# Where the squares of x lie, when the row of norms is laid out, and three small changes of order and banks, in a fused attention block

## The chip, the core and the metric

The kernel runs on one core of a Trainium2 chip. The metric is the device time of one execution in microseconds, median of the runs. TensorE multiplies matrices into the banks of PSUM; ScalarE (ACT), VectorE (DVE) and GpSimd (POOL) work on tiles in SBUF, the first two on PSUM too; SyncE (SP), ScalarE and GpSimd issue DMA transfers.

## The reference

All inputs are float32: 512 positions, model width 1024, 16 heads of 64.

```python
h = rms_norm(x, norm_g)
proj = h @ w_in                     # fq fk fv fz | mq mk mv mz | ga gb | fl
q, k = rms_norm(heads(fq), fox_q_g), rms_norm(heads(fk), fox_k_g)
y_fox = fox_attention(q, k, heads(fv), log_sigmoid(fl + b_f)) * silu(fz)
q, k = rope(rms_norm(heads(mq), moba_q_g)), rope(rms_norm(heads(mk), moba_k_g))
y_moba = moba_attention(q, k, heads(mv)) * silu(mz)
merged = sigmoid(ga + b_gate[0]) * (y_fox @ w_fox) + sigmoid(gb + b_gate[1]) * (y_moba @ w_moba)
return x + merged @ w_out
```

`rms_norm` divides by the root of the mean square plus 1e-6. Both attentions are causal over the 512 positions.

## The kernel before

Every large product is made of three matmuls on split operands: a left and a right operand are each cut into a rounded high part and a low part (`hi`, `lo`; `Gh`, `Gl`; `Zh`, `Zl`), and high by high, high by low and low by high are added in PSUM. ScalarE makes the high part of a tile with a copy, VectorE the low part with a subtraction.

PSUM has eight banks, handed out under tags: `pj` (2 banks), `tp` (3), `lg` (2) and `pv` (1). In SBUF the tag `y` has 15 tiles of 128x512 and the tag `u` has 4. A tile of a tag waits until the oldest one under that tag is free.

The stages, in order of time:

- **Start.** Input tiles of x transposed (`xt`, tag `y`) and the first weights are loaded on SP's queue. Meanwhile TensorE runs `WARM` matmuls on a tile of zeros (L107). Then come two projections that need no norm of x: `first_qk("fqa")` into two `pj` and two `lg` banks, and `first_qk("fka")` into three `tp` banks and `pv`. Each has eight steps `kk` over the inner dimension, with 12 matmuls a step.
- **Norms of x.** `x_stats` (L221) loads x untransposed in eight tiles of 128x512, squares each on ScalarE with a running sum per row (`ms2`), and makes `r`, one over the root, with three small VectorE steps and a power on GpSimd. `norm_row` (L237) lays `r` out as a row over the free dimension (`rbc`) with four transposes on TensorE. `normalise` (L243) multiplies the `xt` tiles with it and splits them into `Gh`, `Gl`.
- **fz gates** (`pz_fza`, `pz_fzb`, L405 to L407), the value projection `fva`, then four attention groups with four heads each. A group is a list of steps `Tr`, `Aa` (logits and exponentials), `Bb` (transposed probabilities times values) and a last step `Yp(1)`, called `gate` in the main loop, which multiplies the group's second pair of heads with its gate and splits it. It is run inside the next group. Projections of later groups (`pj_...`, `pz_...`, `pf`) are woven between the steps as filler.
- **Gates and merging**, with half-size products in a Strassen-like scheme, and at last the output projection, seven products that share sums in the banks `b[1]` to `b[4]` (`product`, L925; `keep`, `result`, L942 to L958). `result` adds the x it needs and sends the rows out: one transfer per tile, and for the very last tile two halves, the second on SP's queue.

The program is written in this order, and a scheduler orders each engine's instructions by its own costs; `issue_after` holds a few back. Each engine runs its list strictly in order. DMA transfers from ScalarE and SP go round eight semaphores: a transfer waits until the one eight places before it has landed.

In the main loop, the step list of a group is put together so:

```python
    for n in range(4):
        ...
        inter(body + ([following] if n < 3 else []) + tail, fill)
        if n < 3:
            body, tail = nxt[1][:1] + gate + nxt[1][1:], nxt[2]
            gate = nxt[3]
```

Of the kernel before, what the change touches and what calls it, by code (L numbers as in the profile page):

```python
# [9 lines left out]
AF = mybir.ActivationFunctionType  # L10
OP = mybir.AluOpType
# [5 lines left out]
NT = S // P  # L17
KT = D // P
HD = 64
CW = 256  # L20
EPS = 1e-6
NEG = -3.0e38
WARM = 8
WR = 4

C_NG, C_BG, C_FQ, C_FK, C_MQ, C_MK, C_BF, C_GQ, C_GK, C_END = 0, 8, 24, 25, 26, 27, 28, 36, 52, 68
# [3 lines left out]
def fox_moba_kernel(ctx: ExitStack, tc, xT, x, w_in, w_fl, w_fox, w_moba, w_out, cst, rope, out):  # L30
# [3 lines left out]
    V, A, G, T = nc.vector, nc.scalar, nc.gpsimd, nc.tensor  # L34
# [182 lines left out]
    r = con.tile([P, NT], F32, name="r")  # L217
# [3 lines left out]
    def x_stats():  # L221
        G.memset(mh, -0.5)
        for t in range(NT):
            for hf in range(2):
                xt = t2("y", 15, f"x{t}{hf}")
                nc.sync.dma_start(out=xt, in_=x[t * P:(t + 1) * P, hf * 512:(hf + 1) * 512])
                j = t2("u", 4, "junk")
                A.activation(j, xt, AF.Square, accum_out=ms2[:, t, hf:hf + 1])
        V.tensor_add(mm, ms2[:, :, 0], ms2[:, :, 1])
        V.tensor_scalar(mm, mm, 1.0 / D, EPS, op0=OP.mult, op1=OP.add)  # L230
        V.tensor_scalar(e2, mm, EPS, None, op0=OP.mult)
        G.tensor_tensor(out=r, in0=mm, in1=mh[:, :NT], op=OP.pow)
# [634 lines left out]
    def group_o():  # L867
        R, B, b, e = {}, {}, {}, {}
        base = len(preps)

        def src(key, c):
            k0, n0 = 4 * (int(key[0]) - 1) + 2 * c, 2 * (int(key[1]) - 1)
            return w_out[n0:n0 + 2, :, k0:k0 + 2, :].rearrange("n p k c -> p n (k c)")

        def wide(t):
            return t.rearrange("p a b -> p (a b)")[:, 0:1024]

        def dst(key, c):
            return wide(R[key, c]).rearrange("p (n k) -> p n k", n=2)

        def load(key, c, pool=sb):
            tag, bufs = ("wr", WR) if pool is sb else ("wx", 4)
            R[key, c] = pool.tile([P, 4, CW], F32, name=f"wr_o{key}{c}", tag=tag, bufs=bufs)
            nc.sync.dma_start(out=dst(key, c), in_=src(key, c))

        def minus(key, c, plus):
            A.activation(R[key, c], R[key, c], AF.Copy, scale=-1.0)  # L887
            G.dma_start(out=dst(key, c), in_=src(plus, c), accum_op=OP.add)  # L888

        def sub(key, c, x, y):  # L890
            V.tensor_tensor(out=wide(R[key, c]), in0=wide(R[x, c]), in1=wide(R[y, c]), op=OP.subtract)

        def prep(n, c):

            def go():
                key = ("11", "21", "22", "12", "22", "11", "21")[n]
                if (n, c) == (2, 0):
                    hi, lo = (stage["pool"].tile([P, 4, CW], F32R, name=f"w{q}_o{n}{c}") for q in "hl")
                else:
                    hi, lo = (sb.tile([P, 4, 264], F32R, name=f"w{q}_o{n}{c}", tag=f"w{q}", bufs=4) for q in "hl")  # L900
                A.activation(wide(hi), wide(R[key, c]), AF.Copy)  # L901
                V.tensor_tensor(out=wide(lo), in0=wide(R[key, c]), in1=wide(hi).bitcast(F32), op=OP.subtract)  # L902
                B[n, c] = [wide(t).rearrange("p (n k c) -> p n k c", n=2, c=CW) for t in (hi, lo)]
                if n == 0:
                    minus("11", c, "12")
            return go
        for key in ("11", "21"):
            for c in range(2):
                loads.append((lambda key=key, c=c: load(key, c), base + 13))
        groups["prep"] = lambda n, cs=(0, 1): [prep(n, c)() for c in cs]  # L910

        def late_loads():
            for key in ("22", "12"):
                for c in range(2):
                    load(key, c, stage["pool"])
            for c in range(2):
                minus("12", c, "22")

        def left_o(what, k, t):
            if what[0] == "S":  # L920
                return [so(what, q)[:, k, t * P:(t + 1) * P] for q in range(2)]
            t0 = HT * (int(what[1]) - 1) + t * P
            return [z[:, t0:t0 + P] for z in MG[4 * (int(what[2]) - 1) + k]]

        def product(n):  # L925
            what, _, at = O_PRODUCTS[n]
            new = at not in b
            if new:
                b[at] = [pst(tg, nb, f"po{at}{t}") for t, (tg, nb) in enumerate(
                    {1: (("lg", 2), ("lg", 2)), 2: (("tp", 3), ("tp", 3)), 3: (("pj", 2), ("pj", 2)),  # L930
                     4: (("tp", 3), ("pv", 1))}[at])]
            for t in range(2):
                o = b[at][t].rearrange("p (n c) -> p n c", n=2)
                for k in range(4):
                    hi, lo = B[n, k // 2]
                    gh, gl = left_o(what, k, t)
                    r = k % 2
                    T.matmul(o, gh, hi[:, :, r, :], start=(new and k == 0), stop=False, skip_group_check=True)  # L938
                    T.matmul(o, gh, lo[:, :, r, :], start=False, stop=False, skip_group_check=True)  # L939
                    T.matmul(o, gl, hi[:, :, r, :], start=False, stop=(k == 3), skip_group_check=True)  # L940

        def keep(at, tq, cq):  # L942

            e[at] = sb.tile([P, 2, S], F32, name=f"eo{at}", tag="qk", bufs=4)
            for t in range(2):
                A.activation(e[at][:, t, :], b[at][t], AF.Copy)
                t0 = tq * HT + t * P
                G.dma_start(out=e[at][:, t, :], in_=x[t0:t0 + P, cq * 512:(cq + 1) * 512], accum_op=OP.add)

        def result(bb, ee, tq, cq, parts=1):  # L950
            for t in range(2):
                o = t2("u", 4, "ot")
                t0 = tq * HT + t * P
                n = 512 // (parts if t else 1)
                for c in range(0, 512, n):
                    V.tensor_tensor(out=o[:, c:c + n], in0=b[bb][t][:, c:c + n], in1=e[ee][:, t, c:c + n], op=OP.add)
                    eng = nc.scalar if c == 0 else nc.sync
                    eng.dma_start(out=out[t0:t0 + P, cq * 512 + c:cq * 512 + c + n], in_=o[:, c:c + n])  # L958

        def evac(n):  # L960
            if n == 0:
                keep(1, 0, 0)
            elif n == 1:
                result(2, 1, 0, 0)
            elif n == 2:
                keep(4, 0, 1)
            elif n == 3:
                keep(3, 1, 1)
            elif n == 4:
                b[6] = b[1]  # L970
                keep(6, 1, 0)
            elif n == 5:
                pass
            else:
                result(3, 6, 1, 0, 2)

        groups["out"] = result
        groups["product"], groups["evac"] = product, evac
        groups["sub"] = lambda *key: [sub(key[0], c, *key[1:]) for c in range(2)]
        groups["WO"] = late_loads  # L980
# [52 lines left out]
    load_fl("fka", COLS["fka"], 0)  # L1033
    load_fl("fka", COLS["fka"], 1)
    b1 = first_qk("fqa", (("pj", 2), ("pj", 2), ("lg", 2), ("lg", 2)))
    b2 = first_qk("fka", (("tp", 3), ("tp", 3), ("tp", 3), ("pv", 1)))
    x_stats()
    for t in range(NT):
        evac_qk(b1[t], "fqa", t)
    for t in range(NT):  # L1040
        evac_qk(b2[t], "fka", t)
    forget_exp()
    norm_row()
    pump(0)
    fz = filler(["fza", "fzb"])
    for k, u in enumerate(fz):
# [14 lines left out]
    for n in range(4):  # L1061
        nxt = []

        def following(n=n, nxt=nxt):
            br, half, cq, ck = plan[n + 1][:4]
            if n == 1:
                moba_begin()
            nxt.extend(attn_group(br, half, col(cq), col(ck)))
            nxt[0][0]()
        fill = filler(plan[n][4])  # L1070
        if n == 0:
            for k in range(4):
                store = []

                at = 3 * k + 5

                def with_sums(u=fill[at], k=k, store=store):
                    u()
                    with tc.issue_after(last_on(mybir.EngineType.DVE)):
                        store.append(make_sums(k))  # L1080

                def with_store(u=fill[at + 1], store=store):
                    u()
                    store[0]()
                fill[at], fill[at + 1] = with_sums, with_store
        inter(body + ([following] if n < 3 else []) + tail, fill)
        if n < 3:
            body, tail = nxt[1][:1] + gate + nxt[1][1:], nxt[2]
            gate = nxt[3]
    seq(["wf3"])  # L1090
    enter("gates")
# [127 lines left out]
```

## Time and profile before

| | |
|---|---|
| median of 3 runs | 426.72 us (426.54 to 426.73) |
| profiled execution | 427.16 us, its span 425.3 us |
| TensorE busy | 418.5 us, 98% of the span |
| VectorE, ScalarE, GpSimd busy | 327.2, 271.4, 98.4 us |
| granted TensorE clock | 1.00 |
| DMA | 58.21 MB, mean 137 GB/s |

The profile gives for each engine the instructions in order of time: start and length in microseconds, engine, line of the kernel, operation, output and inputs by name, shape, count, and in brackets the time for which the engine sat idle before it and what ended that. A matmul's length includes the way through the array, so matmuls in a stream overlap; the distance between their starts is their pace. Rows of windows give, for a stretch of time, its length, then for TensorE, its weight loads, VectorE, ScalarE and GpSimd the busy time and the number of instructions, then the granted clock, the DMA share and GB/s. Rows of waits give the waiting engine and tile, what ended the wait, the total, the count and the longest. A row of one line of the kernel has the smallest, median and largest duration in ns and the first and last start.

### The profile page before, as it was taken

To read this page: it belongs to the slowest core of one execution; us is meant where nothing else is said; L and a number is where in the kernel's file an instruction comes from. 1 tells how busy PE (TensorE), PEld (TensorE's weight loads), DVE (VectorE), ACT (ScalarE), POOL (GpSimd) and SP (SyncE) were. 2 spreads that over 40 slices of the span, in tenths; PEclk is the share of its full clock that TensorE was granted. 3 is DMA by queue.
4 is the path that set the end of the run, shared out by engine and by line. 5 is a ranking of instruction groups with operands and counts; after the bars stand their busy time and mean duration, and the time that the engine had idled before them with its cause. 6 is when DMAs were issued, how large, how long until landed. Compare 5 with 4: busy or idle time off the path is not lost.

```text
span 425.3 us, 7669 instructions
## 1 busy us (share of the span) xinstructions
PE 418.5 (98%) x2887; PEld 387.7 (91%) x2887; DVE 327.2 (77%) x570; ACT 271.4 (64%) x514; POOL 98.4 (23%) x120
## 2 busy tenths in 40 slices
PE   7999999999999999999999999999999999999996
PEld 6998899999999998899998878899999989988884
DVE  5669976769979769568767698767979698689973
ACT  4975436776868867568746687655656535686450
POOL 1048200225132850025750102140000000022140
PEclk9999999999999999999999999999999999999999
DMA  7981144235576334304124222463052603696484
GB/s 243 398 308 55 52 146 139 58 124 175 168 221 217 85 99 125 96 29 125 38 88 124 79 70 72 201 225 123 25 176 65 229 5 112 220 245 116 99 140 158
DMA packets 25621, 58.21 MB, mean 137 GB/s; under 512 B 3064, under 2 KB 7856, under 8 KB 25584
## 3 DMA queue, kind: packets, MB, share of 16 engines
q1 hardware_dynamic: 13392, 38.11, 27.3%
q10 hardware_dynamic: 8800, 11.21, 8.7%
q0 software_dynamic: 3392, 8.39, 8.5%
q8 instruction: 23, 0.38, 0.3%
q14 instruction: 14, 0.11, 0.1%
HBM read 48.11 MB, written 6.32 MB: 128 GB/s over the span
## 4 chain that ended last, share of the span: by engine, by line
PE 96%; DVE 2%; DMA 1%; issue 0%; ACT 0%; SPq 0%; DVEq 0%; ACTq 0%
PE pb_GB L753 3%; PE pb_GA L753 3%; PE pb_GB L750 3%; PE pb_GA L750 3%; PE pb_GB L752 3%; PE pb_GA L752 3%; PE po L939 3%; PE po L938 3%; PE po L940 3%; PE pv L611 2%; PE pv L610 2%; PE lg L556 2%; PE lg L555 2%; PE pm L681 2%; PE pm L680 2%; PE pm L679 2%
## 5 line engine op out<-in xcount | busy, mean ns | idle before, releaser
L560 ACT ACTIVATE p<-p,negm 128x128 f32<-128x128 f32 (+1 forms) x64 | 35.7, 559 | 9.8 <-DVE negm L558 8.6
L558 DVE CUSTOM_DVE_ANT_0 p<-lg,mask 128x128 f32<-128x128 f32 (+1 forms) x64 | 30.9, 485 | 14.3 <-PE lg L556 13.7
L334 POOL TENSOR_TENSOR ff<-ss,mh 128x8 f32<-128x8 f32 x16 | 26.7, 1678 | 65.2 <-DVE ss L332 64.7
L888 POOL DMA_DIRECT2D wr_o<-in_w_out_dram x4 | 4.9, 1293 | 95.5 <-ACT wr_o L887 95.5
L136 DVE TENSOR_TENSOR wl_GA<-wr_ga,wh_GA 128x1024 fp32r<-128x1024 f32 x14 | 17.8, 1288 | 5.8 <-ACT wh_GA L134 3.7
L901 ACT ACTIVATE wh_o<-wr_o 128x1024 fp32r<-128x1024 f32 x14 | 14.8, 1059 | 10.0 <-PE pb_GB L752 2.8
L134 ACT ACTIVATE wh_GB<-wr_gb 128x1024 fp32r<-128x1024 f32 x14 | 14.6, 1059 | 9.5 <-PE pm L680 3.5
L134 ACT ACTIVATE wh_GA<-wr_ga 128x1024 fp32r<-128x1024 f32 x14 | 14.6, 1059 | 9.3 <-PE pb_GA L752 4.6
L555 PE MATMUL lg<-KH,QS 128*128 128x128 f32 (+1 forms) x64 | 20.5, 329 | 0.0
L902 DVE TENSOR_TENSOR wl_o<-wr_o,wh_o 128x1024 fp32r<-128x1024 f32 x14 | 16.9, 1221 | 3.8 <-ACT wh_o L901 3.8
L136 DVE TENSOR_TENSOR wl_GB<-wr_gb,wh_GB 128x1024 fp32r<-128x1024 f32 x14 | 16.9, 1222 | 3.5 <-ACT wh_GB L134 3.5
L636 DVE TENSOR_TENSOR ypair<-pv,ysh 64x512 f32<-64x512 f32 x16 | 11.0, 688 | 11.0 <-ACT ysh L635 10.8
L607 DVE TENSOR_TENSOR ptl<-p_a,pth 128x512 fp32r<-128x512 f32 x16 | 11.0, 685 | 4.6 <-ACT pth L606 4.5
L529 DVE SCALAR_TENSOR_TENSOR QS<-p_qT,cs,QS 64x512 fp32r<-64x512 f32 x16 | 12.0, 750 | 2.5 <-ACT QS L528 2.1
L635 ACT ACTIVATE ysh<-pv 64x512 f32<-64x512 f32 x16 | 9.5, 593 | 6.7 <-PE pv L611 5.6
L753 PE MATMUL pb_GA<-Gh,wl_GA 128*128 128x256 f32 x48 | 13.6, 283 | 0.0
L752 PE MATMUL pb_GA<-Gl,wh_GA 128*128 128x256 f32 x48 | 13.5, 281 | 0.0
L750 PE MATMUL pb_GA<-Gh,wh_GA 128*128 128x256 f32 x48 | 13.5, 281 | 0.0
L753 PE MATMUL pb_GB<-Gh,wl_GB 128*128 128x256 f32 x48 | 13.5, 281 | 0.0
L752 PE MATMUL pb_GB<-Gl,wh_GB 128*128 128x256 f32 x48 | 13.4, 281 | 0.0
L679 PE MATMUL pf<-yhf,wh_wf 128*128 128x512 f32 x32 | 13.1, 408 | 0.4 <-DVE zs_mzb L425 0.4
L528 ACT ACTIVATE QS<-p_qT,cs 64x512 fp32r<-64x512 f32 x16 | 10.9, 681 | 3.8 <-PE lg L555 2.0
(458 smaller groups left out, 1785.9 us busy)
## 6 DMA issues: line engine op xcount, KB each, us to landing
wr_ga<-in_w_in_dram SPq DMA_DIRECT2D x8, 512.0 KB, 3.7
wr_gb<-in_w_in_dram SPq DMA_DIRECT2D x8, 512.0 KB, 5.1
wr_o<-in_w_out_dram SPq DMA_DIRECT2D x8, 512.0 KB, 5.1
xt<-in_xT_dram SPq DMA_DIRECT2D x8, 256.0 KB
x<-in_x_dram SPq DMA_DIRECT2D x8, 256.0 KB, 6.3
KH<-KH ACTq DMA_DIRECT2D x16, 128.0 KB, 2.4
s_dramh<-sum_sh ACTq DMA_DIRECT2D x8, 256.0 KB
s_draml<-sum_sl ACTq DMA_DIRECT2D x8, 256.0 KB, 3.6
```

The source lines that it names most:

```text
L134: A.activation(hi[:, :, 0:n], src, AF.Copy)
L136: eng.tensor_tensor(out=lo[:, q, 0:n], in0=src[:, q], in1=hi[:, q, 0:n].bitcast(F32), op=OP.subtract)
L334: G.tensor_tensor(out=f2, in0=ss.rearrange("p t h -> p (t h)"), in1=mh, op=OP.pow)
L555: T.matmul(lg[:, :n], qs[:, qt], kh[:, :n], start=True, stop=False)
L558: V.tensor_tensor_reduce(pt, lg[:, :n], mask[:, 512 - n:512], -0.125, 3.0e38, op0=OP.add, op1=OP.min, accum_out=mkn[:, hh, i:i + 1])
L560: A.activation(pt, pt, AF.Exp, bias=mkn[:, hh, i:i + 1], scale=-1.0, accum_out=rs[:, hh, i:i + 1])
L679: T.matmul(p, hi[:, k, cc], yh, start=(k == 0), stop=False)
L750: T.matmul(o, hi[:, k, cc], lh, start=(n < 3 and c == 0 and k == 0), stop=False, skip_group_check=True)
L752: T.matmul(o, hi[:, k, cc], ll, start=False, stop=False, skip_group_check=True)
L753: T.matmul(o, lo[:, k, cc], lh, start=False, stop=(k == 3), skip_group_check=True)
L901: A.activation(wide(hi), wide(R[key, c]), AF.Copy)
L902: V.tensor_tensor(out=wide(lo), in0=wide(R[key, c]), in1=wide(hi).bitcast(F32), op=OP.subtract)
```

## The change

- `WARM` is 10 instead of 8.
- In `x_stats` the Square writes over the tile that it reads, so the scratch tile `junk` (tag `u`) is gone; the last two of the eight tiles of x take tag `u` instead of `y`.
- `norm_row()` is called before `first_qk("fka")` instead of after the evacuation of both projections and `forget_exp`.
- In the output projection, the second tile of bank 3 becomes two half tiles in two banks (the third from tag `tp`): its 12 matmuls of 512 columns in each of the two products become 24 of 256 columns, first half and then second half. `keep` and `result` read the halves from their banks.
- `gate` is put behind the second step of the next group's body instead of behind the first.

```diff
-WARM = 8
+WARM = 10
...
             for hf in range(2):
-                xt = t2("y", 15, f"x{t}{hf}")
+                xt = t2("u", 4, f"x{t}{hf}") if t == NT - 1 else t2("y", 15, f"x{t}{hf}")
                 nc.sync.dma_start(out=xt, in_=x[t * P:(t + 1) * P, hf * 512:(hf + 1) * 512])
-                j = t2("u", 4, "junk")
-                A.activation(j, xt, AF.Square, accum_out=ms2[:, t, hf:hf + 1])
+                A.activation(xt, xt, AF.Square, accum_out=ms2[:, t, hf:hf + 1])
...
-                    {1: (("lg", 2), ("lg", 2)), 2: (("tp", 3), ("tp", 3)), 3: (("pj", 2), ("pj", 2)),
+                    {1: (("lg", 2), ("lg", 2)), 2: (("tp", 3), ("tp", 3)), 3: (("pj", 2), ("pj", 2), ("tp", 3)),
                      4: (("tp", 3), ("pv", 1))}[at])]
-            for t in range(2):
-                o = b[at][t].rearrange("p (n c) -> p n c", n=2)
+
+            for t, c in ((0, slice(0, 2)),) + (((1, slice(0, 1)), (1, slice(1, 2))) if at == 3 else ((1, slice(0, 2)),)):
+                o = b[at][t + c.start].rearrange("p (n c) -> p n c", n=2)[:, 0:c.stop - c.start, :]
                 for k in range(4):
...
-                    T.matmul(o, gh, hi[:, :, r, :], start=(new and k == 0), stop=False, skip_group_check=True)
+                    T.matmul(o, gh, hi[:, c, r, :], start=(new and k == 0), stop=False, skip_group_check=True)
...
             for t in range(2):
-                A.activation(e[at][:, t, :], b[at][t], AF.Copy)
+                if at == 3 and t:
+                    for c in range(2):
+                        A.activation(e[at][:, t, c * CW:(c + 1) * CW], b[at][t + c][:, :CW], AF.Copy)
+                else:
+                    A.activation(e[at][:, t, :], b[at][t], AF.Copy)
...
-                    V.tensor_tensor(out=o[:, c:c + n], in0=b[bb][t][:, c:c + n], in1=e[ee][:, t, c:c + n], op=OP.add)
+                    V.tensor_tensor(out=o[:, c:c + n], in0=b[bb][t + 1][:, :n] if c else b[bb][t][:, :n], in1=e[ee][:, t, c:c + n], op=OP.add)
...
     b1 = first_qk("fqa", (("pj", 2), ("pj", 2), ("lg", 2), ("lg", 2)))
-    b2 = first_qk("fka", (("tp", 3), ("tp", 3), ("tp", 3), ("pv", 1)))
     x_stats()
     for t in range(NT):
         evac_qk(b1[t], "fqa", t)
+    norm_row()
+    b2 = first_qk("fka", (("tp", 3), ("tp", 3), ("tp", 3), ("pv", 1)))
     for t in range(NT):
         evac_qk(b2[t], "fka", t)
     forget_exp()
-    norm_row()
...
-            body, tail = nxt[1][:1] + gate + nxt[1][1:], nxt[2]
+            at = 2
+            body, tail = nxt[1][:at] + gate + nxt[1][at:], nxt[2]
             gate = nxt[3]
```

More of the change, by code (lines that the diff above doesn't have):

```diff
@@ L937, in product @@
                     r = k % 2
-                    T.matmul(o, gh, hi[:, :, r, :], start=(new and k == 0), stop=False, skip_group_check=True)
-                    T.matmul(o, gh, lo[:, :, r, :], start=False, stop=False, skip_group_check=True)
-                    T.matmul(o, gl, hi[:, :, r, :], start=False, stop=(k == 3), skip_group_check=True)
+                    T.matmul(o, gh, hi[:, c, r, :], start=(new and k == 0), stop=False, skip_group_check=True)
+                    T.matmul(o, gh, lo[:, c, r, :], start=False, stop=False, skip_group_check=True)
+                    T.matmul(o, gl, hi[:, c, r, :], start=False, stop=(k == 3), skip_group_check=True)
         def keep(at, tq, cq):
```

## The prediction

> **What bounds the kernel now.** I read the page's busy shares and its chain first, then TensorE's waits, then the windows of the first microseconds and of the end.
>
> ```profile
> span 425.3 us, 7669 instructions
> PE 418.5 (98%) x2887; PEld 387.7 (91%) x2887; DVE 327.2 (77%) x570; ACT 271.4 (64%) x514; POOL 98.4 (23%) x120
> PE 96%; DVE 2%; DMA 1%; issue 0%; ACT 0%; SPq 0%; DVEq 0%; ACTq 0%
> ```
>
> TensorE is busy for 98% of the span and carries 96% of the chain that ended last. So a change counts only if it alters the number or the pace of matmuls, opens or closes a gap in their stream, or moves the stretch behind the last one. The gaps are few:
>
> ```profile
> PE warm_ps L107 <- DVE fg_pre L471: 1.5, 1, 1.5
> PE fqa L382 <- ACT Zh L125: 0.7, 1, 0.7
> PE pf L679 <- DVE zs_mzb L425: 0.4, 1, 0.4
> PE p_b L600 <- DVE ptl L607: 0.2, 1, 0.2
> ```
>
> Besides 2.8 us of gaps there are 3.9 us after the last matmul and, hidden inside "busy", the slow pace at the start:
>
> ```profile
> 6.04:9.50 3.46, 3.46 (x16) 3.46 (x17) 3.17 (x6) 2.56 (x4) 0.00 (x0) 1.00 1.02 355
> 9.50:19.00 9.50, 9.50 (x82) 9.50 (x82) 7.54 (x12) 8.19 (x18) 0.00 (x0) 1.00 1.05 397
> 421.40:425.30 3.90, 0.00 (x0) 0.00 (x0) 0.76 (x2) 0.00 (x0) 0.00 (x0) 1.00 0.25 87
> ```
>
> The first entry after the length is TensorE's busy time with its matmuls. In 6.04 to 9.50 it is full with 16 matmuls of 256 columns, 0.216 us each; from 9.50 it is full with 82, 0.116 us each. TensorE ran at about half pace until then, though the granted clock (third from the end) reads 1.00 in both rows. These rows show the turn:
>
> ```profile
> 1.55 3.78 PE L107 MATMUL warm_ps<-warm 128*128 128x512 f32 x8 [1.55 <-DVE fg_pre L471]
> 6.04 0.58 PE L382 MATMUL fqa<-wh_fqa,Zh 128*128 128x256 f32 x1 [0.71 <-ACT Zh L125]
> 9.20 0.41 PE L382 MATMUL fqa<-wh_fqa,Zh 128*128 128x256 f32 x1
> 9.41 0.36 PE L383 MATMUL fqa<-wl_fqa,Zh 128*128 128x256 f32 x1
> 9.61 0.29 PE L382 MATMUL fqa<-wh_fqa,Zh 128*128 128x256 f32 x1
> 19.06 0.53 PE L382 MATMUL fka<-wh_fka,Zh 128*128 128x264 f32 x3
> 30.75 0.39 PE L405 MATMUL pz_fza<-Zh,wh_fza 128*128 128x512 f32 x1
> ```
>
> **Ten warm matmuls instead of eight.** Eight take 1.55 to 5.33, about 0.43 us each (0.21 us per 256 columns, doubled). Two more end at 5.33 + 0.86 = 6.19, while the first real matmul cannot start before 6.04. Their own cost is therefore at most 0.15 us, and less, since a matmul starts before the one ahead has drained. What they fill is the gap of 0.71 us. The fast pace came at about 9.57, some 3.5 us after the gap; the 3.78 us of work before the gap had not brought it. If it takes one stretch of 3.4 us or so without a hole, at fixed places in time, then the stretch before the one that ended at 9.57 ran from about 2.75 to 6.16 and had the gap in it. Without the gap the pace would double at 6.16.
>
> [...]
>
> What an early turn is worth is set by the operands:
>
> ```profile
> 6.59 0.75 DVE L126 SCALAR_TENSOR_TENSOR Zl<-xt,cs,Zh 128x512 fp32r<-128x512 f32 x1
> 9.04 1.43 DVE L126 SCALAR_TENSOR_TENSOR Zl<-xt,cs,Zh 128x512 fp32r<-128x512 f32 x2
> ```
>
> In the changed program's built order, step 0 has 8 matmuls before the first that needs Zl0. At 0.117 us they are issued by 6.98; Zl0 is ready at 7.34, so the other four run 7.4 to 7.9. Step 1's twelve end at 9.3. In step 2 the third matmul already needs Zl2, ready at 9.04 + 0.75 = 9.79, so it starts at 9.84. From there 70 matmuls of this group remain: 9.84 + 70 x 0.117 = 18.0, where the second group starts at 19.06 now. I take 0.1 us off for the two restarts: **-0.9 us** (bounds -1.1 and 0).
>
> **Mean squares and the row of norms.** These are not on TensorE's path, but they could get there.
>
> ```profile
> 19.20 1.07 SPq L226 DMA_DIRECT2D x<-in_x_dram  x1
> L228 ACT ACTIVATE junk<-x x8: 615/630/640, 16.7 to 27.5; 128x512 f32<-128x512 f32 x8
> 18.20 0.74 ACT L313 ACTIVATE qn_fqa<-fqa 128x256 f32<-128x256 f32 x2
> 21.81 0.63 ACT L228 ACTIVATE junk<-x 128x512 f32<-128x512 f32 x1
> 27.46 0.63 ACT L228 ACTIVATE junk<-x 128x512 f32<-128x512 f32 x1 [1.02 <-DMA x<-in_x_dram]
> 28.09 1.14 ACT L327 ACTIVATE sq<-qn_fqa 128x512 f32<-128x512 f32 x2
> 28.22 0.16 DVE L229 TENSOR_TENSOR mm<-ms 128x4 f32<-128x4 f32 x1 [0.52 <-ACT junk L228]
> 28.97 1.04 POOL L232 TENSOR_TENSOR r<-mm,mh 128x4 f32<-128x4 f32 x1
> L240 PE MATMUL p_rbc<-ident,r x4: 272/273/273, 35.7 to 36.0; 128*128 128x128 f32 x4
> L407 PE MATMUL pz_fzb<-Zh,wl_fzb x16: 392/394/399, 42.8 to 53.3; 128*128 128x512 f32 x16
> ```
>
> The eighth tile of x has no buffer until a first Square has freed one, is issued at 19.20, behind weight loads, and is squared at 27.46; r is there at 30.01 and its four transposes run at 35.7. Changed, that tile is issued right behind the seventh, ahead of the weights, and waits only for its queue slot. The seventh is squared at 21.81; the window row at 397 GB/s makes 256 KB 0.66 us, so the eighth is there by 22.5. ScalarE's eight Squares (0.63 us each), four evacuations (0.37) and two other squares (0.57), from 16.7 on, make 7.7 us and end at about 24.4; 0.75 us from the first small DVE step to GpSimd's start (28.22 to 28.97) and 1.04 us make r ready near 26.2. The built order has the four transposes after 76 of the second group's 96 matmuls: 19.06 + 76 x (30.75 - 19.06)/96 = 28.3, or 27.4 with the early pace. They wait for nothing, by 1.2 to 2.1 us, and cost what they did later: 0. SP's weight loads come 0.66 us later; the second group (11.7 us) hides that. Two to four weight chunks wait on DVE behind the earlier row steps; the gate groups, from 30.75 to 53.3, hide those. In-place Squares cost the same.
>
> **Banks.** In the two products into bank 3, 12 matmuls of 512 columns become 24 of 256.
>
> ```profile
> 420.76 0.39 PE L939 MATMUL po<-wl_o,mg 128*128 128x512 f32 x1
> 420.99 0.39 PE L940 MATMUL po<-wh_o,mg 128*128 128x512 f32 x1
> 421.41 0.76 DVE L956 TENSOR_TENSOR ot<-po,eo 128x256 f32<-128x256 f32 x2 [1.39 <-PE po L940]
> 422.20 0.36 SPq L958 DMA_DIRECT2D out_dram<-ot  x1
> L956 DVE TENSOR_TENSOR ot<-po,eo x9: 415/681/692, 399.6 to 421.8; 128x512 f32<-128x512 f32 x7, 128x256 f32<-128x256 f32 x2
> ```
>
> A 512 pair costs 0.23 us, two 256 pairs 0.232 to 0.236: 0.03 us per product, **+0.06**. Now both half adds wait for the last matmul, and the final DMA is issued 1.21 us after that one starts (422.20 - 420.99). Changed, the first half's sum is done twelve matmuls (1.4 us) earlier. The last matmul has 256 columns: 0.28 us (the 9.61 row's 0.29), then one add of 0.42 and 0.06 us of hand-over make 0.76. It starts 0.115 us later in the stream than a 512 one would, so the DMA goes out 1.21 - 0.76 - 0.115 = 0.33 us sooner against an unchanged stream: **-0.33** (bounds -0.2 and -0.6, should the two output DMAs no longer share their landing). The extra ScalarE copy in keep (some 0.15 us) has no one waiting within a microsecond.
>
> **The gate step one place later.** In the last attention group:
>
> ```profile
> 244.31 0.69 DVE L425 SCALAR_TENSOR_TENSOR zs_mzb<-sg,pz_mzb 128x512 f32<-128x512 f32 x1
> 245.05 0.50 PE L679 MATMUL pf<-yhf,wh_wf 128*128 128x512 f32 x1 [0.37 <-DVE zs_mzb L425]
> 248.16 0.67 DVE L607 TENSOR_TENSOR ptl<-p_a,pth 128x512 fp32r<-128x512 f32 x1
> 248.98 0.63 PE L600 MATMUL p_b<-ident,p 128*128 128x128 f32 x4 [0.19 <-DVE ptl L607]
> 249.36 0.67 DVE L425 SCALAR_TENSOR_TENSOR zs_mzb<-sg,pz_mzb 128x512 f32<-128x512 f32 x1
> ```
>
> Built, the second zs_mzb stands right behind the first, so TensorE runs pf0 and pf1, 24 matmuls or 5.6 us, in one piece where p_b stood after 12. The first wait stays; the second goes: -0.2 by its row, -0.4 if the drain of the matmul ahead is counted too. Late next: the last head's pv matmuls near 280, before which the order leaves 12 gate matmuls instead of 19, so 0.8 us less cover. I take **-0.25** (bounds -0.9, both waits gone, and +0.5, new ones of that size).
>
> **Sum.** -0.9 + 0.06 - 0.33 - 0.25 = -1.42 us. The profiled execution took 427.16 us (425.3 us of span and 1.86 around it); it would take 425.74. It stands 0.44 above the median of 426.72, so the median becomes **425.3**.
>
> **The rivals.**
> 1. The pace still doubles near 9.6, because windows fall elsewhere in untraced executions or because the turn needs more than the gap closed. For it: 3.78 us of warm work brought nothing. Against it: a full stretch of 3.5 us did, and three executions within 0.19 us do not look like a turn that wanders. Then only -0.52 is left: 426.2, no change by the bound below. Its chance is 0.30. [...]
> 2. Slower: TensorE stands at the four transposes of the row of norms, now inside the second group, because the eighth tile of x still comes late. Behind them 20 matmuls of that group and everything after are queued. It decides once r is later than 27.4 to 28.3. If r stayed at 30.0, the wait would be 1.7 us, or 2.6 with the early pace, against gains of 0.5 or 1.4: +1.2 us, 427.9. Against it: the built order issues that load without a wait for ScalarE. Chance, with any wait of that size between 240 and 283: 0.12.
>
> **How the numbers follow.** A measurement here tells about 0.2%, 0.85 us, from no change. The forecast has 0.58, rival 1 0.30, rival 2 0.12. The forecast with its bounds reaches from 424.4 (0.2 more at the start, 0.27 more at the end, 0.4 in the middle) to 426.1; it is faster by over 0.85 us in nine of ten cases (0.52). Rival 1 is so in two of ten (0.06) and otherwise the same. Rival 2 gives 0.11 slower. So faster 0.58, same 0.31, slower 0.11. To hold eight in ten the range runs over the forecast and rival 1 with its bounds: 424.4 to 427.0; rival 2 stays outside.
>
> **What would show it.** Right: no gap before fqa; matmuls 0.12 us apart from about 6.2, with short waits for Zl0 and Zl2; the second group from about 18.1; r near 26 and p_rbc without a wait near 27.4; no p_b wait near 249; the last DMA issued 0.76 us after the last matmul's start. Wrong: the 0.21 us pace still there at 9, a wait of p_rbc for GpSimd, or new DVE waits of TensorE over 0.5 us.

## The result: 0.36% slower, by a wait in a place where nothing was changed

The changed kernel takes 427.94 us (median of 22 runs, 426.52 to 430.98), the kernel before beside it 426.75 (22 runs, 426.39 to 428.47). The estimated ratio is 1.0036, with a 95% interval of 1.0023 to 1.0049 (by the medians alone it is 1.0028). The prediction said 425.3, faster. The times lie wider apart than before: 15 runs with a mean granted clock of 0.998 or more took 426.5 to 428.9 us, the 7 with 0.996 or less 429.1 to 431.0. The profiled execution is of the second kind (430.98 us). The medians of the two groups are 427.36 and 430.26 us.

The page of after, its first lines and its chain:

```profile
span 429.0 us, 7697 instructions
PE 420.2 (98%) x2913; PEld 390.4 (91%) x2913; DVE 328.4 (77%) x570; ACT 269.2 (63%) x515; POOL 106.2 (25%) x120
PE 91%; DVE 3%; DMA 3%; issue 1%; ACT 0%; SPq 0%; ACTq 0%; DVEq 0%
```

TensorE's waits in it (total, times, longest):

```profile
PE lg L554 <- DMA KH<-KH: 2.1, 1, 2.1
PE warm_ps L107 <- DVE fg_pre L470: 1.5, 1, 1.5
PE fqa L383 <- DVE Zl L126: 1.0, 1, 1.0
PE pf L678 <- DVE zs_mzb L424: 0.3, 1, 0.3
PE p_b L599 <- DVE ptl L606: 0.2, 1, 0.2
```

The first wait is new: TensorE stands 2.1 us for `KH`, the high half of K, of which a DMA copies one half of the partitions into the other. Here is that place in TensorE's timeline:

```profile
120.28 0.33 PE L609 MATMUL pv<-pth,v_fva 128*128 128x384 f32 x1
122.75 0.33 PE L554 MATMUL lg<-KH,QS 128*128 128x128 f32 x1 [2.15 <-DMA KH<-KH]
123.61 0.41 PE L305 MATMUL pj_mqa<-wh_mqa,Gh 128*128 128x256 f32 x1
123.82 0.41 PE L306 MATMUL pj_mqa<-wl_mqa,Gh 128*128 128x256 f32 x1
127.06 0.28 PE L306 MATMUL pj_mqa<-wl_mqa,Gh 128*128 128x256 f32 x1
127.18 0.28 PE L307 MATMUL pj_mqa<-wh_mqa,Gl 128*128 128x256 f32 x1
```

The records of the granted clock begin at 7.39 us in this trace, and the clock changes at 123.44, at 126.86 and, behind the last instruction, at 430.64 us: 34, 1 and 89 times 3.413 us lie between these points. In before they begin at 9.57 and the next change is at 426.00, again behind the last instruction and 122 times 3.413 us later. A piece of that length, counted from such a point, is called a stretch of the clock here. In windows that follow the stretches (length; busy time of PE, PEld, DVE, ACT, POOL; granted clock; DMA share; GB/s):

```profile
116.62:120.03 3.41, 3.41 (x31) 3.41 (x30) 3.31 (x5) 2.45 (x5) 0.00 (x0) 1.00 0.99 249
120.03:123.44 3.41, 1.26 (x11) 1.01 (x10) 2.46 (x6) 1.01 (x2) 0.00 (x0) 1.00 1.04 266
123.44:126.86 3.42, 3.42 (x19) 3.42 (x18) 2.19 (x9) 1.29 (x5) 1.16 (x1) 0.50 0.18 53
126.86:130.27 3.41, 3.41 (x31) 3.41 (x30) 1.14 (x2) 2.40 (x5) 3.17 (x6) 1.00 0.20 65
```

The wait does a second harm. It leaves TensorE 1.26 us of work in the stretch from 120.03, and through the next stretch the granted clock is 0.50: matmuls of 256 columns start 0.21 us apart (123.61, 123.82) and not 0.12 (127.06, 127.18). Half of 3.42 us, 1.71 us, is lost there. With the wait's 2.15 that makes 3.86 us, a little more than the 3.7 by which the span is longer (429.0 against 425.3); the end gives some back.

Whether the copy comes later or its reader comes sooner is read from the issues of DMAs and from the copies' landings. In the timeline of before, the copy and the matmul that reads it:

```profile
116.98 0.49 ACTq L532 DMA_DIRECT2D KH<-KH  x1
127.43 0.22 PE L555 MATMUL lg<-KH,QS 128*128 128x128 f32 x1
```

The tile `KH` of before, for the four of its sixteen copies whose landing this view can tell (issued at 167.87, 196.95, 227.28 and 245.50):

```profile
DMA to landing us min/median/max: 2.2/2.4/3.9
```

The timeline of after, ScalarE's and SyncE's issues:

```profile
112.80 0.37 ACTq L274 DMA_DIRECT2D s_dramh<-sum_sh  x1
114.80 0.37 ACTq L274 DMA_DIRECT2D s_draml<-sum_sl  x1
115.29 0.40 ACTq L274 DMA_DIRECT2D s_dramh<-sum_sh  x1
115.78 0.52 ACTq L531 DMA_DIRECT2D KH<-KH  x1
115.93 3.96 SPq L207 DMA_DIRECT2D wr_mza<-in_w_in_dram  x2
```

Before, 10.4 us lay between the issue of the copy and the first logit matmul that reads it. After, the copy goes out 1.2 us earlier, yet the matmul's turn comes 4.7 us behind it (120.28 + 0.17, where the next start is due, less 115.78).

The copy itself is slow in both kernels. In the traces of before and after, this copy's semaphore gets sixteen updates behind the issue (in after from 120.57 to 122.71 us); the last of them is taken for the landing. By it, this copy landed at 122.89 before, 5.9 us after its issue, and at 122.71 after, 6.9 us after its issue and 0.04 us ahead of the matmul. In all other traces in which ScalarE issues it, it took between 4.6 and 7.2 us. In each of them a load of 1 MB (`wr_mza`, in two pieces) is under way beside it. The stores of sums of 256 KB ahead of it in ScalarE's queue have come closer, two of them to within the last 1 us; the last of them landed at 118.30, while before all stores issued ahead of the copy had landed by 115.63. Yet the copies of the two traces differ by only 1.0 us, so the stores are at most a small part of the lateness. What changed most is the lead: with 4.7 us, even the copy of before would have come 1.2 us too late.

In the built order, which is the order that the scheduler wrote, the second attention group's first two logit matmuls stand 66 places earlier on TensorE than before (the warm matmuls not counted), now ahead of `p_cc`. No line of the change speaks of them; the scheduler, which plans by its own costs, has moved them.

### The profile page after: what moved, and what is told of

Read it like the earlier page. It is cut to its first block, busy times and chain, and to the rows that moved or that the text cites. A ratio compares the mean times of both kernels' runs of the same rounds, so it can differ in the third digit from the quotient of the medians.

```text
span 429.0 us, 7697 instructions
## 1 busy us (share of the span) xinstructions
PE 420.2 (98%) x2913; PEld 390.4 (91%) x2913; DVE 328.4 (77%) x570; ACT 269.2 (63%) x515; POOL 106.2 (25%) x120
## 4 chain that ended last, share of the span: by engine, by line
PE 91%; DVE 3%; DMA 3%; issue 1%; ACT 0%; SPq 0%; ACTq 0%; DVEq 0%
PE pb_GB L752 3%; PE pb_GA L752 3%; PE pb_GB L749 3%; PE pb_GA L749 3%; PE pb_GB L751 3%; PE pb_GA L751 3%; PE po L940 3%; PE po L939 3%; PE po L938 3%; PE lg L555 2%; PE pv L610 2%; PE lg L554 2%; PE pv L609 2%; PE pf L678 2%; PE pm L680 2%; PE pf L680 2%
## 5 line engine op out<-in xcount | busy, mean ns | idle before, releaser
L333 POOL TENSOR_TENSOR ff<-ss,mh 128x8 f32<-128x8 f32 x16 | 30.5, 1908 | 77.0 <-DVE ss L331 49.9
L136 DVE TENSOR_TENSOR wl_GA<-wr_ga,wh_GA 128x1024 fp32r<-128x1024 f32 x14 | 16.9, 1223 | 4.7 <-ACT wh_GA L134 3.9
L327 DVE TENSOR_REDUCE ss<-sq 128x8 f32<-128x512 f32 x16 | 10.9, 680 | 5.9 <-ACT sq L326 5.9
L554 PEld LDWEIGHTS lg<-KH,QS 128*128 128x128 f32 x64 | 12.1, 189 | 3.1 <-DMA KH<-KH 2.4
L749 PE MATMUL pb_GB<-Gh,wh_GB 128*128 128x256 f32 x48 | 13.3, 281 | 0.0
```

Source lines behind the costliest of these rows:

```text
L136: eng.tensor_tensor(out=lo[:, q, 0:n], in0=src[:, q], in1=hi[:, q, 0:n].bitcast(F32), op=OP.subtract)
L333: G.tensor_tensor(out=f2, in0=ss.rearrange("p t h -> p (t h)"), in1=mh, op=OP.pow)
L554: T.matmul(lg[:, :n], qs[:, qt], kh[:, :n], start=True, stop=False)
L749: T.matmul(o, hi[:, k, cc], lh, start=(n < 3 and c == 0 and k == 0), stop=False, skip_group_check=True)
```

## Experiments

Theory: the harm is this wait and the half clock behind it, and the early place of the logit matmuls comes from three parts together (warm matmuls, tiles of x, row of norms), since only with all three does the built order have it. No run undoes the tiles of x alone; for that part the claim rests on the built order. Rivals: the gate step, which was moved in this very list; or the start.

**e1: the copy of K on another queue.** The edit moves two copies, one for each head of the second group's first pair. The orders of TensorE and VectorE stay as in after.

```diff
-nc.scalar.dma_start(out=kh[ot, :].bitcast(F32), in_=kh[me, :].bitcast(F32))
+(nc.sync if (br, half, pr) == ("f", "b", 0) else nc.scalar).dma_start(out=kh[ot, :].bitcast(F32), in_=kh[me, :].bitcast(F32))
```

> The changed kernel with one thing altered: the two copies of the high halves of K for the second attention group's first pair of heads are issued by SyncE and not by ScalarE, so they do not stand behind ScalarE's stores of the sums (256 KB each). The order of TensorE and of VectorE is the same as in the changed kernel. Wait theory (TensorE stands 2.1 us at 120.6 us for that copy, and the hole halves its clock for one stretch of 3.4 us, about 1.7 us more): both go, no wait of lg over 0.3 us, granted clock 1.00 throughout, and the time falls from 427.9 to 426.5, with runs as close together as those of the kernel before. Rival (the hole is only where other lateness shows, such as the moved gate step or the early row of norms): TensorE waits about as long a little later, for p_cc or the next pv, and the time stays at 427.5 to 428 with the same spread.

Measured: 426.06 us (425.29 to 426.23, 11 runs), 0.9978 of before (0.9970 to 0.9987), 0.4 us below what I expected. From its timeline, SyncE's issue and TensorE's rows:

```profile
114.35 0.53 SPq L531 DMA_DIRECT2D KH<-KH  x1
119.51 0.33 PE L609 MATMUL pv<-pth,v_fva 128*128 128x384 f32 x1
119.68 0.22 PE L554 MATMUL lg<-KH,QS 128*128 128x128 f32 x1
```

The window behind them:

```profile
122.28:125.69 3.41, 3.41 (x31) 3.41 (x31) 2.82 (x7) 2.81 (x9) 1.96 (x2) 1.00 0.44 154
```

With TensorE's order unchanged, the hole and the half clock are gone, and all 11 runs have a granted clock of 0.998 or more. Nothing else took the wait's place. The copy went out 1.4 us earlier than in after, ahead of the load, and landed 3.0 us after its issue (117.39, by its semaphore). The edit changed the queue and the moment of issue together, so it does not tell which of them made the copy quick. It does show what the lateness cost: 1.9 us by the medians, and without it the change is a gain.

**e2, e3, e4: one part of the change undone.**

```diff
 e2: norm_row() after forget_exp() again, first_qk("fka") ahead of x_stats()
 e3: WARM = 8
 e4: body, tail = nxt[1][:1] + gate + nxt[1][1:], nxt[2]
```

> The changed kernel with the row of norms back behind the second projection group and the gate columns; all else as changed. Wait theory: the built order then puts the second group's first two logit matmuls 66 places later on TensorE, behind the p_cc transposes, so the copy of K has landed: no wait there, no half clock, 426.3 to 426.7. Gate theory (the step moved by one place does the harm): 427.9, unchanged. Start theory (the harm comes from warming ten matmuls and the loads of the start): 427.9, unchanged.

> The changed kernel with eight warm matmuls again; all else as changed. Wait theory: here too the built order puts the first two logit matmuls of the second group 65 places later, so no wait and no half clock: 426.2 to 426.7, though nothing of the harm would come from the warm matmuls themselves. Gate theory: 427.9. If the early turn of the pace is worth the 0.9 us that I predicted, it is lost here: 427 or more against e2.

> The changed kernel with the gate step back in its old place; all else as changed, and the first logit matmuls of the second group still early. Wait theory: the wait of about 2 us for the copy of K stays, in some executions with a stretch of half clock: 427.5 to 428.5, runs spread over 4 us. Gate theory: the harm goes, 426.3 to 426.7 with runs within 0.6 us.

Measured: e2 425.64 us (425.09 to 426.16; ratio 0.9966, 0.9955 to 0.9976), e3 425.26 (424.96 to 425.31; 0.9961, 0.9948 to 0.9975), e4 429.29 (428.47 to 429.69; 1.0055, 1.0042 to 1.0068). e2 and e3 have no wait of `lg`. e4 keeps it, 1.4 us long:

```profile
PE lg L554 <- DMA KH<-KH: 1.4, 1, 1.4
```

In windows of its own clock stretches:

```profile
119.42:122.83 3.41, 2.01 (x17) 1.77 (x16) 2.70 (x9) 1.91 (x6) 0.00 (x0) 1.00 1.03 277
122.83:126.24 3.41, 3.41 (x31) 3.41 (x31) 2.01 (x6) 1.95 (x6) 2.26 (x2) 1.00 0.04 16
```

So it is not the gate step: undoing it leaves the harm, and undoing either of two parts that have nothing to do with K takes it away. The start as a whole is no rival either: e1 leaves it as it is and takes the harm away. e4's hole is 1.40 us and leaves 2.01 us of work in its stretch; there the clock stays at 1.00. e2 and e3 were faster than I had expected by 0.7 and 0.9 us, and e4 was 0.8 us above its range. The traced run of e4 is its fastest; four of its five runs have a mean granted clock of 1.00 and still took 428.5 to 429.7 us. What those of 429 us and more lost beyond a wait of 1.4 us was not traced.

**e5 to e8: one part alone, added to the kernel before.**

```diff
 e5: WARM = 10
 e6: products into bank 3, keep and result as changed
 e7: the gate step behind the second step, as changed
 e8: x_stats as changed (tiles and Squares), norm_row() in its old place
```

> The kernel before with ten warm matmuls for eight, and nothing else. Prediction's step (the gap in the warm stretch keeps the clock slow; closing it turns the pace one stretch of 3.4 us earlier, worth 0.9 us): 425.8 to 426.2. Load theory (the first projection group waits for its loads, so an earlier full pace is spent on waits for Zl, and the turn moves with the launch anyway): 426.5 to 427.0, no gain, whatever the trace's time of the turn is. The first logit matmuls of the second group stand late in this order, so no wait for K in either case.

> The kernel before with the products into bank 3 split into two banks, and nothing else. Prediction's step: last DMA issued 0.77 us after the start of the last matmul and not 1.21, 24 narrower matmuls cost 0.06 us more: 0.27 to 0.4 us less, 426.4 to 426.6. Rival (the two output DMAs share their landing, so the end does not move): 426.8 to 427.0.

> The kernel before with the gate step one place later in the list of each group, and nothing else. Prediction's step: the wait of p_b for its DVE split near 249 us goes and the first wait of pf stays: 0.2 to 0.4 us less, 426.4 to 426.6. Gate theory of the harm (new waits between 100 and 140 us or near 280): 427.3 or more. The first logit matmuls of the second group stand late in this order (as in the kernel before), so by the wait theory there is no wait for K.

> The kernel before with the Squares written in place and the last two tiles of x in other buffers, and nothing else (the row of norms stays behind the second group in the program). Prediction's step: no one on TensorE's path waits for it: 426.6 to 427.0, no change. Load theory: the tiles of x no longer hold SyncE's weight loads behind a Square, weights come sooner, and the start up to 54 us is 0.3 to 0.9 us shorter: 425.9 to 426.5.

Measured against 426.74 (33 runs of before): e5 427.69, slower (1.0022, 1.0012 to 1.0031); e6 426.46 (0.9995, 0.9986 to 1.0004); e7 426.19 (0.9991, 0.9980 to 1.0002); e8 426.47 (0.9993, 0.9983 to 1.0003). e6 came out as its step of the prediction said, and e7 0.2 us below its range; e8 lies in the range of the load theory, but its interval includes no change, so it decides nothing. Both theories missed e5: two more matmuls on zeros at 5 us made it slower by 0.95 us. In its trace TensorE is not late at 42 us (`pz_fzb` starts at 41.5 us, before at 42.4), but it loses time later, before logit matmuls among others, as at this row of its timeline:

```profile
142.09 0.50 PE L555 MATMUL lg<-KH,QS 128*128 128x512 f32 x1 [0.31 <-DVE negm L558]
```

Its built order differs from that of before by 245 lines of a diff on TensorE. Summed over the distances between starts, beyond the usual pace of each width, e5 loses 1.5 us more than before between 120 and 160 us. So its 0.95 us is the price of the warm matmuls together with the new order, and what in that order costs the time stays open.

A mean granted clock of 0.995 or less also stands at two of the 21 runs of before that were measured beside e1 (428.3 us), at three of the 11 runs of e7 and at one run each of e6 and e8 (427.4 to 428.2 us). Half of a stretch of 3.41 us lost in a span of 425 us makes a mean of 0.996, so by this estimate a mean of 0.995 or less speaks for a stretch at half clock in kernels without the wait for K as well; none of these runs was traced.

**e9, e10: the wait and the clock once more.** e9 is the changed kernel again; e10 has the three parts alone (gate step and banks as before).

> The changed kernel as it is, again, for a second profile and more times. Clock theory (a hole of over half of one clock stretch of 3.4 us halves the clock for the next stretch; the stretches lie elsewhere in each launch): a wait of lg for K of 1 to 2.5 us again; where it fills more than about 60% of one stretch, a half-clock row of 3.41 us follows it and the run is above 429.5; where two stretches share it, no such row and the run is 427 to 428.7. Rival (the half clock has nothing to do with the hole): a half-clock row at another place, or one without a hole before it.

> The kernel before with ten warm matmuls, the tiles of x and the row of norms as changed, and the banks and the gate step as before. Wait theory: these three together bring the first logit matmuls of the second group forward, so the wait for K is there: the time of e4 plus the 0.3 us of the banks, 429 to 429.8. Rival (it takes the gate step or the banks as well): 426.5 or less.

Measured: e9 430.14 us (430.07 to 430.31; 1.0071, 1.0059 to 1.0083), all six runs at a granted clock of 0.994 to 0.996; e10 431.29 (427.68 to 433.02; 1.0079, 1.0051 to 1.0106). Windows of e9 in its own clock stretches:

```profile
119.46:122.87 3.41, 1.00 (x9) 1.00 (x9) 1.96 (x7) 1.02 (x3) 0.00 (x0) 1.00 1.02 262
122.87:126.29 3.42, 3.42 (x18) 3.42 (x17) 2.09 (x7) 1.29 (x6) 1.57 (x1) 0.50 0.12 37
```

And of e10:

```profile
119.13:122.54 3.41, 1.11 (x9) 0.86 (x8) 2.74 (x6) 1.01 (x2) 0.00 (x0) 1.00 1.08 249
122.54:125.95 3.41, 3.35 (x15) 3.35 (x16) 1.96 (x8) 1.28 (x5) 0.00 (x0) 0.50 0.41 127
```

Three traces, counting after's, have a hole that leaves 1.00 to 1.26 us of work in one stretch, and the next one is at half clock; e4's left 2.01 and was not. The three parts suffice for the harm. e10 is 1.5 us above the upper end of what I expected, and e9 2.2 above after's first median; their waits, 2.4 us in both traces, are longer than the 2.1 and 1.4 that I had gone by. By their semaphores the copy took 7.2 us in both. Why it lands later in some runs than in others stays open.

**e11, e12: the price of the warm matmuls with the order held.** e12 is e2 again; e11 is e2 with eight warm matmuls. Their built orders are the same but for the warm matmuls and a few instructions that trade places with near neighbours (20 lines on TensorE, 10 on VectorE and ScalarE).

> The kernel before with the tiles of x, the gate step and the banks as changed, eight warm matmuls and the row of norms in its old place. Its order on all engines is that of e12 but for a handful of neighbouring matmuls, so e12 minus this one is the price of the two warm matmuls alone. Prediction's step: e12 is 0.9 us faster (this one 426.3 to 426.6). Load theory: no difference over 0.2 us, both 425.3 to 425.7.

> The kernel of e2 again (ten warm matmuls, tiles of x, gate step and banks as changed, row of norms in its old place), beside e11 on the same chip. Prediction's step: 0.9 us faster than e11. Load theory: equal to e11 within 0.2 us, 425.3 to 425.7.

Measured: e11 425.29 us (425.06 to 426.74; 0.9962, 0.9947 to 0.9977), e12 425.85 (425.49 to 426.16; 0.9970, 0.9959 to 0.9981). The warm matmuls cost 0.56 us by the medians. The intervals overlap, so the size is rough and a cost of nothing is not excluded; a gain of 0.9 is. The load theory's 0.2 us was missed too. e3 and e11 beat both kernels.

## Why the prediction was wrong, by its own steps

**Mean squares and row of norms: "They wait for nothing ... and cost what they did later: 0".** This is the step that failed: a term put at nothing. Where it looked it was right: `r` is ready at 27.04 (predicted 26.2) and its transposes run at 28.54 without a wait; the Squares in place have a median of 630 ns, as those into `junk` had.

```profile
26.00 1.04 POOL L231 TENSOR_TENSOR r<-mm,mh 128x4 f32<-128x4 f32 x1 [23.65 <-DVE mm L229]
28.54 0.60 PE L239 MATMUL p_rbc<-ident,r 128*128 128x128 f32 x4
```

But a scheduler orders this program, so the step's cost is not bounded by the place of the edit. Two of the three parts that it takes, the tiles of x and the row of norms, belong to this step; together with the warm matmuls they moved the logit matmuls 66 places at 120 us. In place of 0 the runs showed a wait of 2.15 us and 1.71 us of half clock in the traced run, and 1.9 us by the medians (after less e1), of the 2.6 us by which the forecast was short. The new place stood in the built order, and I did not price it: I looked at the order around the edited places and at 240 to 283 us.

**Rival 2** had the right shape, a TensorE wait of about 2 us that ends slower (427.9 forecast, 427.9 measured), but put it at the row of norms, or between 240 and 283 us, at 0.12. That the number agrees is chance: its mechanism did not occur.

**Ten warm matmuls, -0.9.** This term failed too: there was no gain, but a cost of 0.56 us by the medians with the order held (e12 against e11). Its reading of the clock agrees with the one trace that it had, and with others. In before the stretch from 2.74 to 6.16 was busy for 2.71 of 3.42 us, and the next one ran at half pace; in e8 the stretch from 3.28 to 6.69 was busy for 3.10 of 3.41 us, and the next one ran at full pace. The length of 3.4 us and the fixed places in time, which it had assumed, are what the clock's records show (34, 1 and 89 times 3.413 us in after, 122 times in before); rival 1's windows are these stretches, and they do lie elsewhere in each trace. Why there was no gain is seen from when the operands come. Here is the first `fqa` matmul of e3 and then that of e6, both with eight warm matmuls:

```profile
5.39 0.58 PE L381 MATMUL fqa<-wh_fqa,Zh 128*128 128x256 f32 x1
```

```profile
5.66 0.38 PE L382 MATMUL fqa<-wh_fqa,Zh 128*128 128x256 f32 x1 [0.46 <-ACT Zh L125]
```

The gap of 0.71 us in the trace of before was the longest of the six traces that open with eight warm matmuls; in the others the operands come 0.4 to 0.65 us sooner, and two more matmuls stand in their way until 5.9 to 6.0 in seven of the eight traces with ten (5.63 in e5). Nor was the turn at 9.57 typical. The traces have no record of the clock before the turn, which is why its column reads 1.00 there; the records of the full clock begin, and the pace doubles, at 4.92 (e6), 5.12 (e7), 6.67 (e11), 6.69 (e8) and 7.50 us (e3). And an early turn buys little: the second group starts at 18.3 us with the turn at 5.0 (e5) and at 18.2 with it at 7.50 (e3). What the pace gains, waits for `Zl` take back: 0.3 us in e5, 0.6 in e12, 1.0 in after, where the pace doubled at 7.4 and the second piece of weights came 1.35 us later than in the trace of before (VectorE splits it ahead of making `Zl`). I had taken one launch's loads and place of the stretches as the kernel's.

**Banks, -0.27.** Borne out by the trace, and -0.28 alone by the medians, though the interval includes no change. In after the last matmul starts at 425.18, and the last DMA goes out 0.77 us later (predicted 0.76).

```profile
425.18 0.28 PE L940 MATMUL po<-wh_o,mg 128*128 128x256 f32 x1
425.50 0.42 DVE L960 TENSOR_TENSOR ot<-po,eo 128x256 f32<-128x256 f32 x1 [0.88 <-PE po L940]
425.95 0.36 SPq L962 DMA_DIRECT2D out_dram<-ot  x1
```

**Gate step, -0.25.** Within its bounds: -0.55 alone by the medians, though the interval includes no change. In e7 the `p_b` wait is gone from TensorE's waits and the one for `pf` stays (0.3 us), as forecast; nothing new is late near 280.

**Sum.** -1.42 was forecast. The whole change with the copy of K landing early gives -0.88 (e1, 426.06 against 426.94); with eight warm matmuls -1.68 (e3) and, with the row of norms in its old place too, -1.60 (e11). That the last two lie near the forecast is luck: for the parts in them it had -0.52, so -0.9 of it came from a part that gained nothing. Singly, the tiles of x, the banks and the gate step gave -0.27, -0.28 and -0.55, which is 0.5 us short of -1.60; where the rest comes from stays open. One slip in the range changed nothing: the middle step's own bound of -0.9 lies 0.65 below its -0.25, not 0.4.

## What to carry to other kernels

When a scheduler writes the order, price the difference of the built orders over the whole program, above all reads that come closer to the DMA that feeds them: a lead of 10.4 us shrank to 4.7 here, and no engine's busy time showed it. A hole in TensorE's stream can cost almost twice its length (2.15 us cost 3.86 in after), so a small copy that is read soon should be issued early, ahead of bulk transfers; e1's, issued so and from another queue, landed after 3.0 us and not 6.9. One trace's start is one draw of the loads and of the place of the clock's stretches (the turn came between 4.92 and 9.57 us in traces with eight warm matmuls).

## What the hardware did that I had not expected

The granted clock fell behind holes of little more than 2 us, which no term of my forecast had. Holes of 2.15 to 2.41 us that left 29 to 37% of a 3.41 us stretch busy were followed by a whole stretch at 0.50 (three of three traces); one of 1.40 us that left 59% was not, nor was the 1.0 us wait near 8 us in after, which left 70% (2.40 of 3.41 us). The ends of the traces narrow this down. The last matmuls fill 45% of a stretch in e1 and 48% in after; here are these stretches and what follows, first of e1, then of after:

```profile
419.23:422.65 3.42, 1.54 (x13) 1.33 (x12) 0.98 (x3) 0.00 (x0) 0.00 (x0) 1.00 0.46 164
422.65:424.30 1.65, 0.00 (x0) 0.00 (x0) 0.00 (x0) 0.00 (x0) 0.00 (x0) 0.50 0.00 0
```

```profile
423.82:427.23 3.41, 1.64 (x14) 1.44 (x13) 1.08 (x3) 0.00 (x0) 0.00 (x0) 1.00 0.49 173
427.23:429.00 1.77, 0.00 (x0) 0.00 (x0) 0.00 (x0) 0.00 (x0) 0.00 (x0) 1.00 0.01 2
```

So it is throughout the traces of before and after and in the rows of e1, e4, e9 and e10 shown here: a stretch at full clock of which TensorE was busy for 45% or less was followed by 0.50, and one of 48% or more by 1.00. The ends of matmuls are modelled, so the two shares are rough.

The stretches lie at other places in each trace: those with the hole begin at 120.03 us in after, 119.46 in e9, 119.13 in e10 and 119.42 in e4, and with the same eight warm matmuls the turn came between 4.92 and 9.57 us.

The same copy of 128 KB took 4.6 to 7.2 us in 13 traces, beside a load of 1 MB, where four copies like it took 2.2 to 3.9 us at other places of before. It did not take equally long in every run, and the times show it: the same kernel ran at 426.5 to 431.0 us in one set of runs and at 430.1 to 430.3 in another.
